# The first map's softmax sum is taken out in the merge's norm; one vector operation combines the two maps

## The chip, the core and the metric

The kernel runs on one core of a Trainium2 chip. The core has a matrix engine (TensorE, PE in the profile), a vector engine (DVE), a scalar engine (ACT), GpSimd (POOL), and a sync engine (SP) whose queue issues every transfer of this kernel. The metric is the device time of one execution in microseconds. Before the change it was 1486.08 us, the median of three runs (1483.74 to 1489.56).

## What is computed

One step of one encoder layer, for a prompt of 1024 frames and for a sample of 32 frames with 512 cached ones. Both go through one input projection, then through two branches, gated linear attention (GLA) and differential attention, and are merged. Differential attention has 8 heads with two maps each; in each map a query of 64 numbers meets keys of 64, and the second map is subtracted with a learned weight `lam`:

```python
def diff_attend(q, k, v, mask, lam):
    s = jnp.einsum('bqhmd,bkhmd->bhmqk', q, k).astype(F32) * (DIFF_HD ** -0.5)
    if mask is not None:
        s = jnp.where(mask, s, -jnp.inf)
    p = jax.nn.softmax(s, axis=-1)
    attn = p[:, :, 0] - lam * p[:, :, 1]
    return jnp.einsum('bhqk,bkhe->bqhe', attn, v.astype(F32))
```

Each head's output then goes through an RMS norm over its 128 channels, and only after that is it multiplied by its gate:

```python
def rmsnorm(x, g):
    xf = x.astype(F32)
    y = xf * lax.rsqrt(jnp.mean(xf * xf, axis=-1, keepdims=True) + EPS) * g.astype(F32)
    return y.astype(x.dtype)
yd = (rmsnorm(o_diff, diff_subln_g) * (1.0 - lambda_init)) * silu(dg)
merged = sigmoid(ma) * (yg @ w_proj_gla) + sigmoid(mb) * (yd @ w_proj_diff)
```

A factor that all channels of one frame of one head share drops out of this norm, except for the small `EPS`.

## The kernel before

Frames and channels are tiled by 128. Every float matmul of a projection is done as three products of rounded parts (high times high, low times high, high times low), so a block of 128 output channels is 3 chunks of 352 frames with 24 matmuls each, 72 in all. The program runs in stages: the norm and the value projections; GLA; differential attention; the merge (projection of the GLA branch, called PG, projection of the attention branch, called PD, and the output projection).

In the two attention stages the blocks of the input projection serve as **fill**: `fill` (L444) hands out six matmuls at a time (L461 to L463) wherever the attention must wait. The order of PE's instructions is made at build time by the class `Order` (L62): each step has a cost, needs with latencies (the table `W`, L52), and PSUM banks; of the threads the first whose step is ready is taken. The latencies are constants, and none is measured while the kernel runs. The instructions of the other engines are put in order by the framework, by priority.

For each head `diff_main` (L896) runs over 8 query tiles i of 128 frames; tile i has w = 128 (i+1) keys. `diff_scores` (L865) makes the scores of both maps (`ps_s`, L879 and L880), their maxima (L883), and the exponentials with their row sums on ACT (L885, sums in the two columns of `sm`). DVE then inverts both sums (L888), multiplies the second map by its inverse and by -lam (L889, over w columns), and multiplies the first map by its inverse and adds the second (L890, over w columns). The result `p` is ready for PE after the latency `soft + W["p"] + w * W["p_w"]` (L894). PE transposes it in groups of up to four 128x128 blocks (`ps_t`, L927; one PSUM bank, freed by the copies L929 and L930), and every second tile multiplies it with the values (`po`, L940 to L942). The row sums before are used up by this; the outputs `osb` and their squares `sqo` are kept.

`diff_fin` (L851) ends a head: the mean square over channels by a matmul (`ps_m`, L855), its store to `msd` (L858), the gate (L861) and the store to `ydd` (L862). The norm itself is applied in the merge: `msd` is loaded as `rs` (L1127), turned into an inverse root by Ln and Exp (L1128, L1129), stored to `rsd` (L1130), loaded as a broadcast `rsb` for two heads at a time (L1136) and multiplied onto the tiles `ydr` (L1137), which are then split into high and low parts `Y` (L1065, L1066) for PD (L439 to L441).

The sample's 32 frames are a thread of their own, `sample_thread` (L950), in four groups of two heads: scores (`ps_ss`, L982), two transposes (`ps_st`, L1002: four blocks, then a remainder of 32 columns), products (`po_s`, L1014), a scaling (`os_`, L1021) and an output transpose (`ps_so`, L1025). The two kinds of transposes share one PSUM bank. The first two blocks of PG are computed together in steps over the tiles `ygr` as they are loaded and split into `y` (`pg_first`, L1081; L1095 to L1097).

Of the kernel before, what the change touches and what calls it, by code (L numbers as in the profile page):

```python
# [11 lines left out]
F32 = mybir.dt.float32  # L12
F32R = mybir.dt.float32r
I32 = mybir.dt.int32
AF = mybir.ActivationFunctionType
ALU = mybir.AluOpType
# [4 lines left out]
P = 128  # L21
NP = 1024
# [6 lines left out]
DH, HD = 8, 64  # L29
NQ = NP // P  # L30
EPS = 1e-6
# [24 lines left out]
    "tr_t": 2.27, "dv": 5.65, "at": 2.45, "pv_o": 1.1, "sdg": 1.84, "sdk": 21.35, "kc": 7.45, "ss_s": 3.69,  # L56
    "sp": 7.1, "st_t": 1.14, "sv": 3.44, "spt": 0.43, "so_o": 3.58, "so": 4.1, "so_t": 0.72, "yg0": 4.48,
    "yg": 1.18, "pg_b": 1.72, "sm": 1.98, "sm_w": 0.00141, "sm_s": 2.25, "p": 2.4, "p_w": 0.00204,
}


# [61 lines left out]
def hybrid_step_kernel(ctx: ExitStack, tc: tile.TileContext, a):  # L123
    nc = tc.nc
    mm = nc.tensor.matmul
    act = nc.scalar.activation
    ve = nc.vector
    dma = nc.sync.dma_start
    st = nc.sync.dma_start
# [4 lines left out]
    dram = ctx.enter_context(tc.tile_pool(name="dram", bufs=1, space=DRAM))  # L134
# [10 lines left out]
    def tbank(name):  # L145
        return pp.tile([P, 512], F32, tag="t", name=name)
# [5 lines left out]
    ident = cst.tile([P, P], F32, name="ident")  # L152
    make_identity(nc, ident)
    eps = cst.tile([P, 1], F32, name="eps")
# [23 lines left out]
    ptd = dram.tile([KT, P, T], F32, name="ptd")  # L178

    msd = dram.tile([DH, NP], F32, name="msd")  # L180
    rsd = dram.tile([DH, NP], F32, name="rsd")


# [146 lines left out]
    with tc.manual_schedule(engines={E.PE, E.Activation, E.DVE, E.Pool}):  # L330
# [25 lines left out]
        ps = bank("ps_v")  # L356
# [400 lines left out]
    dp = pool("dp", reuse_waits="tile")  # L757
# [19 lines left out]
    def sam(n, h):  # L777
        return smp[:, 20 + 4 * n + h % 4, :]

    dqs, dks, dsg = {}, {}, {}  # L780

    def parts(n, cnt):
# [82 lines left out]
    def diff_scores(h, i, out):  # L865
        w = (i + 1) * P
        qsl = slice(i * P, i * P + P)
        qs, (ks, kls) = dqs[h], dks[h]
        sm = dp.tile([P, 2], F32, tag="sm", bufs=2, name="sm")
        pt = []  # L870
        soft = W["sm"] + w * W["sm_w"]
        for m in range(2):
            cost = sum(max(0.11, min(512, w - n0) / 2200) for n0 in range(0, w, 512)) * 2
            yield cost, [(("dk", h), W["dk"]), (("dq", h), W["dq"])], ["s"]
            ps = dbank("ps_s")

            for n0 in range(0, w, 512):
                n = min(512, w - n0)
                mm(ps[:, n0 : n0 + n], qs[m][:, qsl], ks[m][:, n0 : n0 + n], start=True, stop=False)  # L879
                mm(ps[:, n0 : n0 + n], qs[m][:, qsl], kls[m][:, n0 : n0 + n], start=False, stop=True)  # L880
            ve.memset(ps[0:64, w - 64 : w], -1e30)  # L881
            nm = dp.tile([P, 1], F32, tag=f"nm{m}", bufs=2, name="nm")
            ve.tensor_reduce(nm, ps[:, 0:w], axis=AX.X, op=ALU.max, negate=True)  # L883
            p = dp.tile([P, NP], F32, tag=f"p{m}", bufs=2 - m, name="p")
            act(p[:, 0:w], ps[:, 0:w], AF.Exp, bias=nm, accum_out=sm[:, m : m + 1])  # L885
            S.free("s", soft + W["sm_s"])
            pt.append(p)
        ve.reciprocal(sm, sm)  # L888
        ve.tensor_scalar(pt[1][:, 0:w], pt[1][:, 0:w], sm[:, 1:2], neglam, op0=ALU.mult, op1=ALU.mult)  # L889
        ve.scalar_tensor_tensor(pt[0][:, 0:w], pt[0][:, 0:w], sm[:, 0:1], pt[1][:, 0:w], op0=ALU.mult, op1=ALU.add)  # L890
        S.mark(("p", h, i))
        if i == NQ - 1:
            S.mark(("qk", h))
        out[i] = pt[0], soft + W["p"] + w * W["p_w"]  # L894

    def diff_main():  # L896
        fin = None
        for h in range(DH):
            att = {}
            yield 0.0, [(("dq", h), 0.0), (("dk", h), 0.0)], []  # L900
            yield from diff_scores(h, 0, att)
            if fin is not None:
                yield from fin
            vr = tp.tile([P, NQ, P], F32, tag="sg1", name="vr")
            dma(vr, a["newv"][0:NP, h * P : h * P + P].rearrange("(c p) e -> p c e", p=P))
            vh = dp.tile([P, NQ, P], F32R, tag="vh", name="vh")
            vl = dp.tile([P, NQ, P], F32R, tag="vl", name="vl")
            act(vh, vr, AF.Copy)
            nc.gpsimd.tensor_tensor(vl, vr, vh.bitcast(F32), op=ALU.subtract)
            S.mark(("dv", h))  # L910
            osb = tp.tile([P, NP], F32, tag="o", name="osb")
            sqo = rp.tile([P, NP], F32, tag="gst", name="sqo")
            for i in range(NQ):
                g = i // 2
                if i + 1 < NQ:
                    yield from diff_scores(h, i + 1, att)
                p, lat = att.pop(i)
                if i % 2 == 0:
                    ah = dp.tile([P, NQ, 256], F32R, tag="ah", name="ah")
                    al = dp.tile([P, NQ, 256], F32R, tag="al", name="al")  # L920
                dsl = slice((i % 2) * P, (i % 2) * P + P)
                for j0 in range(0, i + 1, 4):
                    nj = min(4, i + 1 - j0)
                    yield 0.11 * nj, [(("p", h, i), lat)], ["t"]
                    ps = tbank("ps_t")
                    for j in range(j0, j0 + nj):
                        nc.tensor.transpose(ps[:, (j - j0) * P : (j - j0 + 1) * P], p[:, j * P : j * P + P], ident)  # L927
                    pv = ps[:, : nj * P].rearrange("p (c s) -> p c s", s=P)
                    act(ah[:, j0 : j0 + nj, dsl], pv, AF.Copy)  # L929
                    ve.tensor_tensor(al[:, j0 : j0 + nj, dsl], pv, ah[:, j0 : j0 + nj, dsl].bitcast(F32),  # L930
                                     op=ALU.subtract)
                    S.free("t", W["tr_t"])
                S.mark(("at", h, i))
                if i % 2 == 0:
                    continue
                yield 0.32 * (i + 0.5), [(("at", h, i), W["at"]), (("dv", h), W["dv"])], ["o"]
                po = obank("po")[:, 0:256]
                for j in range(i + 1):
                    cs = slice(0, 256) if j < i else slice(P, 256)
                    mm(po[:, cs], vh[:, j, :], ah[:, j, cs], start=(j == 0), stop=False)  # L940
                    mm(po[:, cs], vh[:, j, :], al[:, j, cs], start=False, stop=False)  # L941
                    mm(po[:, cs], vl[:, j, :], ah[:, j, cs], start=False, stop=(j == i))  # L942
                act(sqo[:, g * 256 : g * 256 + 256], po, AF.Square)
                act(osb[:, g * 256 : g * 256 + 256], po, AF.Copy)
                S.free("o", W["pv_o"])
                S.mark(("pv", h, g))
            fin = diff_fin(h, osb, sqo)
        yield from fin

    def sample_thread():  # L950
        w = PAST + NS
# [171 lines left out]
    Y = x_pair("Y")  # L1123
    yd = [Y[k // 6][:, k % 6] for k in range(KT)]

    rs = cp.tile([DH, NP], F32, tag="cwh", name="rs")
    dma(rs, msd)  # L1127
    act(rs, rs, AF.Ln, bias=eps[0:DH])  # L1128
    act(rs, rs, AF.Exp, scale=-0.5)  # L1129
    st(rsd, rs)  # L1130
    rsb = {}
# [165 lines left out]
```

## Time and profile before

| | |
|---|---|
| median of three runs | 1486.08 us |
| the profiled execution | 1489.96 us, of it the span 1488.2 us |
| granted PE clock, mean | 0.989 |
| DVE, ACT, POOL busy in the span | 53%, 40%, 20% |
| transfers | 156.58 MB, 32% of the 16 engines' time |
| differential attention on PE | some 605 to 1188 us of the span |
| the merge's first projection (PG) | some 1189 to 1290 us |

The profile is of one execution. Its page has the busy time of each engine, the span in slices, the chain of work that ended last, and the costliest groups of instructions; the trace behind it can be asked for timelines and windows of time. Matmuls overlap: one of 352 columns is listed with some 0.32 us, and the next one starts some 0.16 us after it. An idle time before an instruction is listed with the instruction that ended it.

### The profile page before, as it was taken

How to read it: one execution, taken by the hardware profiler on the slowest of the kernel's cores; microseconds unless marked ns; L12 is line 12 of the kernel's file. 1: busy time of each engine (PE TensorE's matmuls, PEld its weight loads, DVE VectorE, ACT ScalarE, POOL GpSimd, SP SyncE). 2: the span in 40 equal slices, each digit the busy share in tenths (PEclk: the TensorE clock that was granted, in tenths of full speed). 3: DMA queues.
4: the chain of work that ended last, by engine and by line, in shares of the span. 5: the costliest groups of instructions: out<-in, count | busy, mean ns of one | idle time of the engine just before them, and what ended most of it. 6: DMA issues, size and time to landing. Idle time of an engine off the chain costs nothing.

```text
span 1488.2 us, 22365 instructions
## 1 busy us (share of the span) xinstructions
PE 1427.6 (96%) x8848; PEld 1330.4 (89%) x8848; DVE 790.4 (53%) x1464; ACT 600.5 (40%) x1262; POOL 298.4 (20%) x186
## 2 busy tenths in 40 slices
PE   8999999998989999899999999999899899999997
PEld 6787778988989899899989998999799789999997
DVE  5612004565565443576767676768665536455415
ACT  4522114445444233355555555555454432221311
POOL 1200002132312133222222322222221111121001
PEclk9999999999999999999999999999999999999999
DMA  8621111122222134313141323233322278643205
GB/s 295 215 99 38 44 43 45 52 74 70 75 89 66 66 101 124 102 47 119 52 115 62 108 74 105 64 100 85 97 62 86 91 264 311 215 135 127 100 1 191
DMA packets 66742, 156.58 MB, mean 105 GB/s; under 512 B 10008, under 2 KB 28568, under 8 KB 65600
## 3 DMA queue, kind: packets, MB, share of 16 engines
q1 hardware_dynamic: 66624, 155.01, 32.2%
q8 instruction: 74, 1.21, 0.3%
q14 instruction: 44, 0.36, 0.1%
HBM read 104.39 MB, written 40.04 MB: 97 GB/s over the span
## 4 chain that ended last, share of the span: by engine, by line
PE 51%; DVE 5%; DMA 4%; ACT 2%; issue 1%; POOL 1%; SPq 0%; DVEq 0%; POOLq 0%; ACTq 0%
PE ps_w L461 9%; PE ps_w L462 9%; PE ps_w L463 9%; PE ps_w L440 2%; PE ps_w L439 2%; PE ps_w L441 2%; PE ps_c L1189 2%; PE ps_c L1191 2%; PE ps_c L1190 2%; PE ps_s L880 2%; PE ps_t L927 2%; PE ps_s L879 2%; DMA ydr<-ydd 1%; PE po L941 1%; PE po L942 1%
## 5 line engine op out<-in xcount | busy, mean ns | idle before, releaser
L461 PE MATMUL ps_w<-X,wh 128*128 128x352 f32 x1344 | 451.8, 336 | 8.4 <-ACT k L492 3.2
L462 PE MATMUL ps_w<-X,wl 128*128 128x352 f32 x1344 | 437.4, 325 | 0.0
L463 PE MATMUL ps_w<-X,wh 128*128 128x352 f32 x1344 | 435.5, 324 | 0.0
L431 POOL TENSOR_TENSOR wl<-wr,wh 128x1024 fp32r<-128x1024 f32 x72 | 178.5, 2479 | 659.6 <-ACT wh L429 535.9
L461 PEld LDWEIGHTS ps_w<-X,wh 128*128 128x128 f32 x1344 | 255.3, 190 | 13.5 <-issue 4.8
L462 PEld LDWEIGHTS ps_w<-X,wl 128*128 128x128 f32 x1344 | 255.3, 190 | 1.2 <-issue 1.2
L463 PEld LDWEIGHTS ps_w<-X,wh 128*128 128x128 f32 x1344 | 256.0, 190 | 0.0
L885 ACT ACTIVATE p<-ps_s,nm 128x256 f32<-128x256 f32 (+7 forms) x128 | 94.6, 741 | 58.7 <-DVE ps_s L881 31.0
L286 PE MATMUL ps_v<-wh,X 128*128 128x512 f32 x248 | 98.1, 396 | 1.9 <-DVE X L225 1.9
L285 PE MATMUL ps_v<-wh,X 128*128 128x512 f32 x248 | 99.5, 401 | 0.0
L287 PE MATMUL ps_v<-wl,X 128*128 128x512 f32 x248 | 98.9, 399 | 0.0
L429 ACT ACTIVATE wh<-wr 128x1024 fp32r<-128x1024 f32 x72 | 75.8, 1053 | 55.1 <-PE ps_w L463 30.4
L883 DVE TENSOR_REDUCE nm<-ps_s 128x1 f32<-128x256 f32 (+7 forms) x128 | 94.7, 746 | 2.7
L272 DVE TENSOR_TENSOR vo<-ps_v,vo 32x512 f32<-32x512 f32 x4 | 2.7, 678 | 141.7 <-ACT vo L271 141.7
L881 DVE MEMSET ps_s<- 64x64 f32 x128 | 14.3, 112 | 114.7 <-PE ps_s L880 113.1
L646 POOL TENSOR_TENSOR vl<-vr,vh 128x512 fp32r<-128x512 f32 (+1 forms) x20 | 24.8, 1238 | 223.9 <-ACT vh L645 223.9
L879 PE MATMUL ps_s<-k,q 128*128 128x512 f32 (+2 forms) x192 | 68.0, 362 | 1.2 <-DMA k<-k 1.2
L880 PE MATMUL ps_s<-kl,q 128*128 128x512 f32 (+2 forms) x192 | 63.9, 348 | 3.7 <-DMA kl<-kl 3.2
L268 ACT ACTIVATE vo<-ps_v 128x512 f32<-128x512 f32 x32 | 19.1, 596 | 116.5 <-PE ps_v L287 115.6
L929 ACT ACTIVATE ah<-ps_t 128x512 fp32r<-128x512 f32 (+2 forms) x96 | 46.9, 488 | 43.8 <-PE ps_t L927 43.1
L930 DVE TENSOR_TENSOR al<-ps_t,ah 128x512 fp32r<-128x512 f32 (+2 forms) x96 | 53.1, 553 | 18.7 <-ACT ah L929 17.4
L440 PE MATMUL ps_w<-Y,wl 128*128 128x352 f32 x192 | 62.3, 324 | 0.0
(319 smaller groups left out, 2971.0 us busy)
## 6 DMA issues: line engine op xcount, KB each, us to landing
wr<-w SPq DMA_DIRECT2D x72, 512.0 KB
thd<-gate SPq DMA_DIRECT2D x16, 528.0 KB
xn<-xn SPq DMA_DIRECT2D x16, 512.0 KB
wr<-wv SPq DMA_DIRECT2D x16, 512.0 KB
newk<-rr SPq DMA_DIRECT2D x8, 528.0 KB
ygr<-ygd SPq DMA_DIRECT2D x8, 528.0 KB
tha<-thd SPq DMA_DIRECT2D x8, 528.0 KB
ydr<-ydd SPq DMA_DIRECT2D x8, 528.0 KB
```

The source lines that it names most:

```text
L285: mm(ps, xk[:, 0, t0 : t0 + P], wh[:, k, :], start=(k == 0), stop=False)
L286: mm(ps, xk[:, 1, t0 : t0 + P], wh[:, k, :], start=False, stop=False)
L287: mm(ps, xk[:, 0, t0 : t0 + P], wl[:, k, :], start=False, stop=(k == KT - 1))
L431: nc.gpsimd.tensor_tensor(wl, wr, wh.bitcast(F32), op=ALU.subtract)
L440: mm(ps[:, :n], wl[:, k, :], src[k][:, 0, t0 : t0 + n], start=False, stop=False)
L461: mm(ps[:, :n], wh[:, k, :], src[k][:, 0, t0 : t0 + n], start=(k == 0), stop=False)
L462: mm(ps[:, :n], wl[:, k, :], src[k][:, 0, t0 : t0 + n], start=False, stop=False)
L463: mm(ps[:, :n], wh[:, k, :], src[k][:, 1, t0 : t0 + n], start=False, stop=(k == KT - 1))
L879: mm(ps[:, n0 : n0 + n], qs[m][:, qsl], ks[m][:, n0 : n0 + n], start=True, stop=False)
L880: mm(ps[:, n0 : n0 + n], qs[m][:, qsl], kls[m][:, n0 : n0 + n], start=False, stop=True)
L883: ve.tensor_reduce(nm, ps[:, 0:w], axis=AX.X, op=ALU.max, negate=True)
L885: act(p[:, 0:w], ps[:, 0:w], AF.Exp, bias=nm, accum_out=sm[:, m : m + 1])
```

## The change

The exponentials of the first map are no longer divided by their sum. The second map is scaled by -lam times the first map's sum over its own, a number for each frame, and one operation multiplies and adds. What goes to the values is therefore the old map times the first map's sum s0, and so is the head's output. The sums s0 of all heads and tiles are gathered in the 64 columns of one tile `s0a`, transposed at the end of the attention, and stored. In the merge the mean square (s0 squared times the old one) gets EPS times s0 squared in place of EPS, which makes the norm's result the old one. The sample is computed as before. Two numbers of the planner's table change: the latency from the exponentials to the transposes.

```diff
-    ... "p": 2.4, "p_w": 0.00204,
+    ... "p": 2.2, "p_w": 0.00145,
...
+    s0d = dram.tile([DH, NP], F32, name="s0d")
...
+    s0a = tp.tile([P, DH * NQ], F32, name="s0a")
+    s0t = tp.tile([DH * NQ, P], F32, name="s0t")
...
-        sm = dp.tile([P, 2], F32, tag="sm", bufs=2, name="sm")
+        sm = dp.tile([P, 1], F32, tag="sm", bufs=2, name="sm")
+        s0 = s0a[:, h * NQ + i : h * NQ + i + 1]
...
-            act(p[:, 0:w], ps[:, 0:w], AF.Exp, bias=nm, accum_out=sm[:, m : m + 1])
+            act(p[:, 0:w], ps[:, 0:w], AF.Exp, bias=nm, accum_out=sm if m else s0)
...
         ve.reciprocal(sm, sm)
-        ve.tensor_scalar(pt[1][:, 0:w], pt[1][:, 0:w], sm[:, 1:2], neglam, op0=ALU.mult, op1=ALU.mult)
-        ve.scalar_tensor_tensor(pt[0][:, 0:w], pt[0][:, 0:w], sm[:, 0:1], pt[1][:, 0:w], op0=ALU.mult, op1=ALU.add)
+        ve.scalar_tensor_tensor(sm, sm, neglam, s0, op0=ALU.mult, op1=ALU.mult)
+        ve.scalar_tensor_tensor(pt[0][:, 0:w], pt[1][:, 0:w], sm, pt[0][:, 0:w], op0=ALU.mult, op1=ALU.add)
...
         yield from fin
+        yield 0.11, [], ["t"]
+        ps = tbank("ps_s0")
+        nc.tensor.transpose(ps[0 : DH * NQ, 0:P], s0a, ident)
+        act(s0t, ps[0 : DH * NQ, 0:P], AF.Copy)
+        S.free("t", W["tr_t"])
+        st(s0d.rearrange("h (i q) -> (h i) q", q=P), s0t)
...
-    rs = cp.tile([DH, NP], F32, tag="cwh", name="rs")
+    rs2 = cp.tile([DH, 2, NP], F32, tag="cwh", name="rs")
+    rs, s0 = rs2[:, 0], rs2[:, 1]
     dma(rs, msd)
-    act(rs, rs, AF.Ln, bias=eps[0:DH])
+    dma(s0, s0d)
+    ve.scalar_tensor_tensor(s0, s0, EPS, s0, op0=ALU.mult, op1=ALU.mult)
+    ve.tensor_tensor(rs, rs, s0, op=ALU.add)
+    act(rs, rs, AF.Ln)
     act(rs, rs, AF.Exp, scale=-0.5)
```

With the two numbers of the table the order of PE's instructions changes. Three places follow. Line numbers of the changed kernel are higher: L462 to L464 are the fill (before L461 to L463), L1013 the sample's transposes (before L1002).

The first is on PE, at the end of the sixth head and the start of the seventh, for the third group of the sample. Before, its two transposes (`ps_st`) stood there with six fill matmuls and a mean-square matmul between them:

```order
L879 MATMUL ps_s<-k_11286,q_10924 128x128
L880 MATMUL ps_s<-kl_11288,q_10924 128x128
L1002 MATMUL ps_st<-ident,p 128x128 x4
L461 MATMUL ps_w<-X_89,wh 128x352
L462 MATMUL ps_w<-X_89,wl 128x352
L463 MATMUL ps_w<-X_89,wh 128x352
L461 MATMUL ps_w<-X_89,wh 128x352
L462 MATMUL ps_w<-X_89,wl 128x352
L463 MATMUL ps_w<-X_89,wh 128x352
L855 MATMUL ps_m<-sqo,one_h 128x512
L1002 MATMUL ps_st<-ident,p 32x128
```

Now, for the same group, the second transpose stands behind the last product of the seventh head and the next head's first scores:

```order
L947 MATMUL po<-ah,vl 128x256
L945 MATMUL po<-ah,vh 128x128
L946 MATMUL po<-al,vh 128x128
L947 MATMUL po<-ah,vl 128x128
L883 MATMUL ps_s<-k_12105,q_11699 128x128
L884 MATMUL ps_s<-kl_12107,q_11699 128x128
L883 MATMUL ps_s<-k_12106,q_11700 128x128
L884 MATMUL ps_s<-kl_12108,q_11700 128x128
L1013 MATMUL ps_st<-ident,p 32x128
L462 MATMUL ps_w<-X_89,wh 128x352
```

The first transpose of that group (four blocks) now stands 79 rows ahead of this one, before the last tile's transposes of the seventh head.

The second place is on PE too, at the end of the last head. Before, the transposes of its last tile (`ps_t`, eight blocks) stood between the products of the sample, and the head's last product (`po`) followed at once, without fill:

```order
L463 MATMUL ps_w<-X_89,wh 128x352
L1002 MATMUL ps_st<-ident,p 32x128
L1014 MATMUL po_s<-vcs,smp 32x128 x4
L1015 MATMUL po_s<-smp 32x128
L927 MATMUL ps_t<-ident,p 128x128 x8
L1014 MATMUL po_s<-vcs,smp 32x128 x4
L1015 MATMUL po_s<-smp 32x128
L940 MATMUL po<-ah,vh 128x256
```

Now fill steps stand between those transposes (18 matmuls behind each four blocks), and behind the last product (L945 to L947) there is fill as well, with the sample's last transposes:

```order
L945 MATMUL po<-ah,vh 128x128
L946 MATMUL po<-al,vh 128x128
L947 MATMUL po<-ah,vl 128x128
L1013 MATMUL ps_st<-ident,p 128x128 x4
L462 MATMUL ps_w<-X_89,wh 128x352
L463 MATMUL ps_w<-X_89,wl 128x352
L858 MATMUL ps_m<-sqo,one_h 128x512
L464 MATMUL ps_w<-X_89,wh 128x352
```

The last group's products and output now stand among the first matmuls of the merge.

The third place is the queue of SP in the merge. The norms' way (`rs`, `rsd`, `rsb`) stands among weight loads (`wr`), stores of finished PG blocks (`ptd`) and loads of gates (`tha`). Before:

```order
L1127 DMA rs<-msd 8x1024
L1062 DMA ydr<-ydd 128x1056 x2
L1102 DMA ptd<-tha 128x1056
L427 DMA wr<-w 128x1024
L1130 DMA rsd<-rs 8x1024
L1102 DMA ptd<-tha 128x1056
L1074 DMA tha<-thd 128x1056
L427 DMA wr<-w 128x1024
L1074 DMA tha<-thd 128x1056
L1136 DMA rsb<-rsd 128x2048
```

Now, with the weight load of PG's fourth block already issued ahead of these rows:

```order
L1139 DMA rs<-msd 8x1024
L1085 DMA tha<-thd 128x1056
L1113 DMA ptd<-tha 128x1056
L428 DMA wr<-w 128x1024
L1140 DMA rs<-s0d 8x1024
L1085 DMA tha<-thd 128x1056
L1073 DMA ydr<-ydd 128x1056 x2
L1122 DMA ptd<-tha 128x1056
L1085 DMA tha<-thd 128x1056
L428 DMA wr<-w 128x1024
L1145 DMA rsd<-rs 8x1024
L1151 DMA rsb<-rsd 128x2048
```

The first broadcast stands behind the store of PG's third block and the weight load of the sixth block; before it stood behind the store of the second and the weight load of the fifth.

More of the change, by code (lines that the diff above doesn't have):

```diff
@@ L57 @@
     "sp": 7.1, "st_t": 1.14, "sv": 3.44, "spt": 0.43, "so_o": 3.58, "so": 4.1, "so_t": 0.72, "yg0": 4.48,
-    "yg": 1.18, "pg_b": 1.72, "sm": 1.98, "sm_w": 0.00141, "sm_s": 2.25, "p": 2.4, "p_w": 0.00204,
+    "yg": 1.18, "pg_b": 1.72, "sm": 1.98, "sm_w": 0.00141, "sm_s": 2.25, "p": 2.2, "p_w": 0.00145,
 }
```

## The prediction, made before the changed kernel ran

> **What bounds the kernel now.** The page's first part comes first: the busy time of each engine and its share of the span.
>
> ```profile
> PE 1427.6 (96%) x8848; PEld 1330.4 (89%) x8848; DVE 790.4 (53%) x1464; ACT 600.5 (40%) x1262; POOL 298.4 (20%) x186
> ```
>
> TensorE (PE) is busy 96% of a span of 1488.2 us, so a faster vector engine (DVE) can only shorten the times in which PE stands still for it. The second view is the table of windows, over the three stages that the change reaches: the differential attention of the prompt, the change-over to the merge, and the first projection of the merge. Columns: window, length, then busy time and instructions of PE, weight loads, DVE, ACT, POOL, then the granted clock, the DMA share and GB/s.
>
> ```profile
> 610.00:1180.00 570.00, 558.51 (x3583) 528.95 (x3584) 392.20 (x775) 298.05 (x687) 135.76 (x63) 1.00 0.27 80
> 1180.00:1215.00 35.00, 28.18 (x169) 24.97 (x170) 14.79 (x18) 13.51 (x20) 3.08 (x3) 1.00 0.75 258
> 1215.00:1300.00 85.00, 84.24 (x519) 82.94 (x518) 43.05 (x47) 23.77 (x25) 19.08 (x8) 1.00 0.73 266
> ```
>
> PE stands still for 570 - 558.51 = 11.5 us in the attention, 35 - 28.18 = 6.8 us in the change-over and 0.8 us in the projection, with the clock at 1.00. DVE is busy only 392 of 570 us. About 19 us is all that this change can win; its arithmetic on PE stays as it is. The timeline of PE then says where these 19 us lie (start, duration, instruction; in brackets the idle time before it and what ended it).
>
> ```profile
> 754.67 0.28 PE L1002 MATMUL ps_st<-ident,p 128*32 128x128 f32 x1 [1.27 <-DVE smp L1005]
> 792.16 0.33 PE L927 MATMUL ps_t<-ident,p 128*128 128x128 f32 x1 [1.33 <-DVE al L930]
> 1034.99 0.66 PE L927 MATMUL ps_t<-ident,p 128*128 128x128 f32 x4 [1.32 <-DVE al L930]
> 1046.41 0.27 PE L1002 MATMUL ps_st<-ident,p 128*32 128x128 f32 x1 [2.33 <-DVE smp L1005]
> 1073.90 0.63 PE L927 MATMUL ps_t<-ident,p 128*128 128x128 f32 x4 [1.68 <-DVE smp L1028]
> 1181.95 0.66 PE L927 MATMUL ps_t<-ident,p 128*128 128x128 f32 x4 [1.41 <-DVE al L930]
> 1184.29 0.39 PE L940 MATMUL po<-ah,vh 128*128 128x256 f32 x1 [0.36 <-ACT os__13006 L1016]
> 1189.06 0.43 PE L1095 MATMUL ps_w<-y,wh 128*128 128x352 f32 x1 [1.52 <-ACT y L1065]
> 1190.58 0.43 PE L1097 MATMUL ps_w<-y,wh 128*128 128x352 f32 x1 [0.93 <-DVE y L1066]
> 1195.57 0.43 PE L1095 MATMUL ps_w<-y,wh 128*128 128x352 f32 x1 [1.29 <-ACT y L1065]
> 1196.86 0.43 PE L1097 MATMUL ps_w<-y,wh 128*128 128x352 f32 x1 [0.70 <-DVE y L1066]
> ```
>
> None of these rows waits for the two operations that the change edits (L889, L890). The long ones wait for a one-bank transpose buffer that a late DVE operation holds, mostly around the sample's steps (L1002, L1005, L1028), and at the change-over for the loads of the merge.
>
> **The edit on DVE.** The groups by line (count, busy us, mean ns) and three rows of the DVE timeline give its price.
>
> ```profile
> L890 DVE SCALAR_TENSOR_TENSOR p<-p,sm 128x128 f32<-128x128 f32 (+3 forms) x64 | 56.5, 883 | 1.8
> L889 DVE TENSOR_SCALAR p<-p,sm,neglam 128x128 f32<-128x128 f32 (+3 forms) x64 | 43.0, 672 | 1.8
> L888 DVE RECIPROCAL sm<-sm 128x2 f32<-128x2 f32 x64 | 10.4, 163 | 18.1 <-ACT p L885 17.2
> L995 DVE TENSOR_TENSOR r<-r,coef 128x1 f32<-128x1 f32 x4 | 0.9, 233 | 0.1
> ...
> 1046.19 0.33 DVE L889 TENSOR_SCALAR p<-p,sm,neglam 128x128 f32<-128x128 f32 x1
> 1046.55 0.35 DVE L890 SCALAR_TENSOR_TENSOR p<-p,sm 128x128 f32<-128x128 f32 x1
> 1091.64 0.75 DVE L889 TENSOR_SCALAR p<-p,sm,neglam 128x896 f32<-128x896 f32 x1
> ```
>
> Removed: 64 tensor_scalar, 43.0 us. Added: 64 scalar_tensor_tensor on one column, which the trace does not show. Bounds: the reciprocal of two columns, 163 ns, and the 128-column form of the same operation, 0.35 us. I take 233 ns, the one-column tensor_tensor, the nearest in shape and operands: 64 x 0.233 = 14.9 us. DVE is relieved by 43.0 - 14.9 = 28.1 us (20.6 to 32.6). The wide operation that stays keeps its 56.5 us, and the reciprocal its price. The probabilities of a tile are ready earlier by 0.33 - 0.23 = 0.1 us at 128 columns and 0.5 us at 896. Of the 28 us almost nothing lies on the path, since PE has fill matmuls to run meanwhile.
>
> Whether the freed operation ever held DVE up longer shows beside POOL:
>
> ```profile
> 1060.68 2.47 POOL L796 TENSOR_TENSOR sw<-sw,stb 128x1056 f32<-128x1056 f32 x1
> 1060.74 2.50 DVE L1021 TENSOR_SCALAR os__11629<-os__11629,ss 64x128 f32<-64x128 f32 x1 [0.66 <-POOL ss L162]
> 1185.51 0.28 DVE L1021 TENSOR_SCALAR os__13006<-os__13006,ss 64x128 f32<-64x128 f32 x1 [0.66 <-POOL ss L162]
> ```
>
> The same small operation takes 2.50 us beside a POOL operation and 0.28 us alone. [...]
>
> **The order on PE.** The two planner numbers for the latency of the probabilities fall by 0.28 us at 128 columns and 0.80 us at 1024. In each head one fill step of six matmuls leaves the inside of the head, eight in all, to be used later; the sample's steps move too. What that does, term by term:
>
> - The sample's two transposes no longer stand close to each other in the first three groups: many matmuls come between. The waits of 1.27 and 2.33 us go: -3.6 us.
> - At the end of the last head, fill steps now stand between the transposes and behind the last product. The 1.41 us, and 0.36 us for the sample's output, go: -1.7 us.
> - The 1.32 us at 1034.99 comes from a DVE queue that also carries the splits of k. The sample's scores no longer stand there; I count half: -0.7 us.
> - The backlogs around the sample's outputs (1.33, 1.68 us and smaller ones; what remains of the 11.5 us apart from the terms above is 6.6 us) recur in three heads after the change as before. The last such head has no rotation left for POOL and DVE. A shorter queue takes somewhat over a quarter: -1.8 us (0 to -6.6).
> - At the change-over the waits of 1.52, 0.93, 1.29 and 0.70 us remain: the same loads, conversions and splits precede the first product of the merge. The fill moved there covers about 2 us, but the store of the last gate and a weight conversion now stand ahead of the merge's second and third tiles on the sync engine's queue and on ACT. I count 0 (-4.4 to +2).
> - New waits: transposes now come one fill step earlier behind their scores. The narrowest tile of those shows what is left:
>
> ```profile
> 855.47 0.89 DVE L890 SCALAR_TENSOR_TENSOR p<-p,sm 128x640 f32<-128x640 f32 x1
> 858.45 0.60 PE L927 MATMUL ps_t<-ident,p 128*128 128x128 f32 x4
> ```
>
>  The slack is 858.45 - 856.36 = 2.1 us. One fill step is six matmuls; by the two rows under "rivals" one matmul costs 0.16 us, so the transposes come 0.97 us earlier, and 1.1 us stays even without the edit. In two heads the sample's transposes now stand just ahead of the last tile's and hold the one bank. I count +2.0 us for all new waits (0 to +4).
> - The transpose of the sums, one matmul with its bank: +0.3 us. Its copy on ACT and its store have no one waiting nearby.
>
> The sum is -3.6 - 1.7 - 0.7 - 1.8 + 0 + 2.0 + 0.3 = **-5.5 us**.
>
> **The norm in the merge.** Two more loads and vector operations stand ahead of the broadcast of the norms, and the sync engine now issues it behind the weights of a block that is one later. The rows of before:
>
> ```profile
> 1207.49 0.32 SPq L1127 DMA_DIRECT2D rs<-msd  x1
> 1216.05 1.15 ACT L1128 ACTIVATE rs<-rs,eps 8x1024 f32<-8x1024 f32 x1
> 1218.51 1.06 ACT L1129 ACTIVATE rs<-rs 8x1024 f32<-8x1024 f32 x1
> 1225.32 0.38 SPq L1136 DMA_DIRECT2D rsb<-rsd  x1
> 1273.01 1.25 DVE L1066 TENSOR_TENSOR Y<-ydr,Y 128x1056 fp32r<-128x1056 f32 x1
> 1289.93 0.32 PE L439 MATMUL ps_w<-Y,wh 128*128 128x352 f32 x1
> ```
>
> The last tile is split at 1274.3 and used at 1289.9: a cover of 15.6 us. A block is 72 matmuls, 11.6 us. The two added operations are bounded by nothing and by 1.25 us each (the split of 1056 columns). The last tile is then ready at 1285.9 to 1288.4, still 1.5 to 4 us early. Price: nothing, with little cover left.
>
> **Rivals.** (1) The waits only change their place. The planner's numbers fall by some 0.2 us more than the edit saves, and each new order meets POOL's 2.4 us operations at other points. For it: the waits above come from chance meetings; against it: the two longest go by the order alone. It gives -1 us, 1485. (2) The relief of DVE clears nearly all waits for it: -3.6 - 1.7 - 1.3 - 6.6 = -13 us, 1473. Against it: L1021 and the conversions of the merge do not change. (3) Slower: the norm comes a second block late. If the first broadcast misses one more weight load on the sync engine's queue, the last tile is ready at 1297.5 to 1300, PE waits 7.6 to 10 us ahead of the second projection, and the time is 1486.1 - 5.5 + 10 = 1490.6, or 1495 if the waits above remain. It decides from a delay of 15.6 us; I count 11.6 to 14.1. (4) The change doesn't do what it says: all sums lie in one tile, and if each exponential had to wait for the last use of that tile on DVE, 64 tiles would each lose up to 0.5 us, 1486.1 - 5.5 + 32 = 1513. Against it: in the built program the first map's exponential waits for DVE at the same counts as before. (5) PE is not the bound at all:
>
> ```profile
> 1025.88 0.32 PE L463 MATMUL ps_w<-X,wh 128*128 128x352 f32 x1
> 1029.72 0.32 PE L463 MATMUL ps_w<-X,wh 128*128 128x352 f32 x1
> ```
>
> If PE had hidden room as large as the idle time of the weight loads in the attention (570 - 528.95 = 41 us), all of DVE's 28.1 us could come out: 1458. Between these two rows lie 24 starts in 3.84 us, 0.16 us each, at half the duration of a matmul: the stream is dense. [...]
>
> **How the numbers follow.** The profiled execution took 1489.96 us (its span and 1.8 us around it), 3.9 us over the median of 1486.08. The terms are differences made in that execution: 1484.5 for it, and 1486.1 - 5.5 = 1480.6, so 1481, on the median. Chances: forecast (1477.5 to 1483) 0.42, rival 1 0.24, rival 2 0.18, rival 3 0.11, rival 4 0.03, rival 5 0.02. The range 1471 to 1492 takes in rivals 1 and 2 and most of 3 and leaves out the rest. A measurement of this kernel tells about 0.5%, 7.4 us, from no change: faster than 1478.7 are rivals 2 and 5 and a quarter of the forecast, 0.31; slower than 1493.5 are half of rival 3 and rival 4, 0.09; between them 0.60.
>
> **What would show it.** In the changed kernel's timeline of PE the sample's second transposes should have no wait in front, the last head's transposes no wait over 0.5 us, and the first four waits of the merge should still sum to 3 to 5 us. DVE's busy time should fall by 20 to 33 us, the one-column operation take 0.16 to 0.35 us. The window 610 to 1180 should show some 5 us of idle PE less. A wait of PE for Y ahead of the second projection would be rival 3. The forecast is wrong if new waits over 1 us stand in the heads around the sample's outputs, or if the merge's first tiles come later than counted.

## The result and the profile after

The changed kernel takes **1502.43 us** (median of 4 runs, 1501.49 to 1504.63); the kernel before took 1486.00 us beside it. The ratio is 1.0103, its 95% interval 1.0078 to 1.0128: slower by 1%. The forecast was 1481, its range 1471 to 1492.

The first part of the page of the changed kernel, with its span, to be held against that of before:

```profile
span 1501.1 us, 22384 instructions
PE 1434.7 (96%) x8849; PEld 1337.4 (89%) x8849; DVE 761.6 (51%) x1466; ACT 599.1 (40%) x1263; POOL 296.8 (20%) x186
```

DVE has 28.8 us less to do, as the change promises. PE has one instruction more and yet is busy 7.1 us longer, and the span is 12.9 us longer. So PE stood still longer (5.8 us of the span), and something made its instructions slower. The windows of the attention and of the change-over show both (columns as before: PE, weight loads, DVE, ACT, POOL, then the granted clock):

```profile
610.00:1190.00 580.00, 560.13 (x3549) 531.39 (x3549) 365.47 (x774) 295.36 (x681) 133.95 (x63) 0.98 0.27 78
1190.00:1225.00 35.00, 31.92 (x185) 27.53 (x184) 14.66 (x16) 13.35 (x23) 3.04 (x2) 0.95 0.66 220
```

In the attention PE now stands still for 19.9 us, where it was 11.5, and the granted clock is 0.98 in place of 1.00. The timeline of PE says where (the idle time ahead of an instruction and its releaser in brackets):

```profile
782.04 0.34 PE L1036 MATMUL ps_so<-ident,os__8566 64*128 64x64 f32 x1 [3.80 <-DVE os__8566 L1032]
857.16 0.63 PE L932 MATMUL ps_t<-ident,p 128*128 128x128 f32 x4 [1.15 <-DVE ps_s L885]
927.90 0.63 PE L932 MATMUL ps_t<-ident,p 128*128 128x128 f32 x4 [1.15 <-DVE ps_s L885]
961.71 1.08 PE L932 MATMUL ps_t<-ident,p 128*128 128x128 f32 x4 [5.05 <-DVE smp L1016]
1044.35 0.30 PE L883 MATMUL ps_s<-k,q 128*128 128x128 f32 x1 [1.56 <-ACT osb L949]
1046.78 0.30 PE L884 MATMUL ps_s<-kl,q 128*128 128x128 f32 x1 [2.12 <-DMA kl<-kl]
1122.94 0.47 PE L884 MATMUL ps_s<-kl,q 128*128 128x128 f32 x1 [2.16 <-DMA kl<-kl]
1200.12 0.43 PE L1106 MATMUL ps_w<-y,wh 128*128 128x352 f32 x1 [1.41 <-ACT y L1076]
```

None of the waits of before that the prediction quoted from 750 to 1182 us is there; in their place stand seven new ones of 17.0 us in all (the first seven rows). The two longest wait for the sample's operations on DVE, two for the remainders of K (`kl`, its low parts) at the start of a head. What the longest wait leaves behind it shows in windows of 2 us; the last three numbers are the clock, the DMA share and GB/s:

```profile
778.00:780.00 2.00, 0.24 (x3) 0.10 (x1) 1.94 (x3) 0.94 (x3) 1.57 (x1) 1.00 0.66 270
780.00:782.00 2.00, 0.00 (x0) 0.00 (x0) 1.90 (x2) 0.00 (x0) 1.02 (x1) 0.78 0.00 0
782.00:784.00 2.00, 1.96 (x7) 1.87 (x8) 0.41 (x2) 0.00 (x0) 0.00 (x0) 0.50 0.84 253
784.00:786.00 2.00, 2.00 (x8) 1.71 (x7) 0.17 (x2) 0.00 (x0) 0.00 (x0) 0.50 0.13 26
786.00:788.00 2.00, 2.00 (x10) 1.90 (x9) 1.79 (x3) 0.12 (x1) 0.00 (x0) 0.51 0.00 0
788.00:790.00 2.00, 2.00 (x14) 2.00 (x13) 0.87 (x2) 2.00 (x4) 0.00 (x0) 1.00 0.00 0
```

PE resumes at 782.0 with the clock at 0.50 and starts 7 to 10 instructions in 2 us where it starts 14 at full clock. Summed as (1 - clock) x 2 us over these rows, 3.4 us are lost, all but 0.4 of them on top of the wait. Such a stretch is called a **fall** below, and what it loses its loss.

Why the 5.05 us? ACT's row for the sample's transposes, and DVE's timeline behind it:

```profile
954.76 0.39 ACT L1015 ACTIVATE smp<-ps_st 128x256 f32<-128x256 f32 x1 [2.80 <-PE ps_st L1013]
```

```profile
953.02 2.76 DVE L801 TENSOR_TENSOR rr<-rr,ct 128x352 f32<-128x352 f32 x3
...
956.67 0.95 DVE L803 TENSOR_TENSOR rr<-rr,sw 128x352 f32<-128x352 f32 x2
957.54 0.41 DVE L834 TENSOR_TENSOR kl<-rr,k 64x256 fp32r<-64x256 f32 x1
...
960.68 0.42 DVE L835 TENSOR_TENSOR kl<-rr,k 64x256 fp32r<-64x256 f32 x1
961.14 0.42 DVE L1016 TENSOR_TENSOR smp<-ps_st,smp 128x256 f32<-128x256 f32 x1
```

The sample's first transposes (954.12 on PE) now come 8 us after the end of the K projection of the next head, just when the rotation of that K reaches DVE. ACT has copied its half by 955.15, but DVE's add (L1016) is queued behind the whole rotation (L801 to L803) and split (L834, L835) of that K, and the bank that it holds is the only one for transposes. The 3.80 us have the same form: the sample's scaling L1032, ready after 773.7, stands behind the next tile's steps, among them four splits of q and one combination of probabilities that takes 2.85 us beside a POOL operation (0.89 us for the same form at 707.74, with none beside it; DVE's timeline, then POOL's):

```profile
778.86 2.85 DVE L895 SCALAR_TENSOR_TENSOR p<-p,sm 128x640 f32<-128x640 f32 x1
781.63 0.27 DVE L1032 TENSOR_SCALAR os__8566<-os__8566,ss 64x128 f32<-64x128 f32 x1
```

```profile
778.43 2.59 POOL L432 TENSOR_TENSOR wl<-wr,wh 128x1024 fp32r<-128x1024 f32 x1 [4.70 <-ACT wh L430]
```

### The profile page after: what moved, and what is told of

The parts are those of the page before. It is cut to its first block, busy times and chain, and to the rows that moved or that the text cites. A ratio compares the mean times of both kernels' runs of the same rounds, so it can differ in the third digit from the quotient of the medians.

```text
span 1501.1 us, 22384 instructions
## 1 busy us (share of the span) xinstructions
PE 1434.7 (96%) x8849; PEld 1337.4 (89%) x8849; DVE 761.6 (51%) x1466; ACT 599.1 (40%) x1263; POOL 296.8 (20%) x186
## 3 DMA queue, kind: packets, MB, share of 16 engines
q8 instruction: 74, 1.21, 0.3%
## 4 chain that ended last, share of the span: by engine, by line
PE 53%; DVE 6%; DMA 4%; ACT 2%; issue 1%; POOL 1%; SPq 0%; DVEq 0%; POOLq 0%; ACTq 0%
PE ps_w L462 9%; PE ps_w L463 9%; PE ps_w L464 9%; PE ps_s L884 2%; PE ps_s L883 2%; PE ps_w L441 2%; PE ps_w L440 2%; PE ps_w L442 2%; PE ps_t L932 2%; PE ps_c L1206 2%; PE ps_c L1204 2%; PE ps_c L1205 2%; DMA kl<-kl 1%; PE po L946 1%; PE ps_m L858 1%; PE po L947 1%
## 5 line engine op out<-in xcount | busy, mean ns | idle before, releaser
L462 PE MATMUL ps_w<-X,wh 128*128 128x352 f32 x1344 | 454.2, 338 | 8.5 <-ACT k L493 3.2
L463 PE MATMUL ps_w<-X,wl 128*128 128x352 f32 x1344 | 438.0, 326 | 0.0
L464 PE MATMUL ps_w<-X,wh 128*128 128x352 f32 x1344 | 436.9, 325 | 0.0
L432 POOL TENSOR_TENSOR wl<-wr,wh 128x1024 fp32r<-128x1024 f32 x72 | 175.2, 2433 | 621.2 <-ACT wh L430 557.3
L462 PEld LDWEIGHTS ps_w<-X,wh 128*128 128x128 f32 x1344 | 256.5, 191 | 14.4 <-issue 5.7
L463 PEld LDWEIGHTS ps_w<-X,wl 128*128 128x128 f32 x1344 | 256.5, 191 | 1.8 <-issue 1.7
L464 PEld LDWEIGHTS ps_w<-X,wh 128*128 128x128 f32 x1344 | 256.7, 191 | 0.2 <-issue 0.2
L440 PE MATMUL ps_w<-Y,wh 128*128 128x352 f32 x192 | 61.7, 321 | 0.0
```

The lines of the kernel that those rows point to most:

```text
L432: nc.gpsimd.tensor_tensor(wl, wr, wh.bitcast(F32), op=ALU.subtract)
L462: mm(ps[:, :n], wh[:, k, :], src[k][:, 0, t0 : t0 + n], start=(k == 0), stop=False)
L463: mm(ps[:, :n], wl[:, k, :], src[k][:, 0, t0 : t0 + n], start=False, stop=False)
L464: mm(ps[:, :n], wh[:, k, :], src[k][:, 1, t0 : t0 + n], start=False, stop=(k == KT - 1))
```

## Experiments

Three theories are told apart. A: the new order of PE, made by the two planner numbers, costs the time, by new waits. B: the new arithmetic costs it. C, beside either: each long wait of PE is followed by a fall of the clock, so that it costs more than it lasts.

**Order or arithmetic.** The first two kernels take the change apart: e1 is the kernel before with the two planner numbers, e2 the changed kernel without them.

```diff
 e1, in the kernel before:
-"p": 2.4, "p_w": 0.00204,
+"p": 2.2, "p_w": 0.00145,
 e2, in the changed kernel: the same lines the other way round
```

> The kernel before with the two planner numbers alone (p 2.2, p_w 0.00145); both maps are still scaled as before. Its TensorE order is that of the changed kernel row for row, save the transpose of the sums. Theory A (the order costs the time): the waits of 3.8 us (sample's output transpose) and 5.05 us (last tile's transposes behind the sample's add) and those for the K remainders stand here too, each followed by a stretch at half clock: 1498 to 1510 us. Theory B (the new arithmetic costs it): 1483 to 1489 us, as before. If 1490 to 1497, each has a part of it.

> The changed kernel with the old planner numbers (p 2.4, p_w 0.00204); the arithmetic, the transpose of the sums and the norm's three added steps in the merge are in. Its TensorE order is that of before row for row, with one transpose more. Theory A: no wait over 3 us between 610 and 1190 us, VectorE busy near 762 us, 1478 to 1488 us. Theory B: 1498 to 1505 us, with the waits of the changed kernel.

Measured: e1 1512.28 us, ratio 1.0176 (1.0160 to 1.0191); e2 1485.83 us, ratio 1.0006 (0.9992 to 1.0019). The mechanism of theory A holds in both, though e1 lies 2 us above its range: the order alone costs 26 us, and the arithmetic is worth nothing in the old order. In the new order it is worth 10 us (1512.3 to 1502.4): the waits of e1 are the same ones, longer (4.92 us in place of 3.80, 2.36 and 2.38 in place of 1.15), apart from that of 5.05 us, which stands there unchanged, and one of 1.56 us at 961 us more. A shorter DVE queue helped only where PE waited for that queue.

**The two long waits.** e3 takes the sample's add and its scaling away from DVE's queue, in the changed kernel:

```diff
-ve.tensor_tensor(pT[0:kw, c0 : c0 + n], pv[:, :, :, 1, :], pT[0:kw, c0 : c0 + n], op=ALU.add)
+p2 = p[0:kw, 0 : n * 64].rearrange("p (c h t) -> p c h t", h=2, t=NS)
+act(p2, pv[:, :, :, 1, :], AF.Copy)
+ve.tensor_tensor(pT[0:kw, c0 : c0 + n], p2, pT[0:kw, c0 : c0 + n], op=ALU.add)
...
-ve.tensor_scalar(os_, os_, ss, None, op0=ALU.mult)
+act(os_, os_, AF.Copy, scale=ss)
```

> The changed kernel and its numbers, with two operations of the sample's thread taken off VectorE's queue: its second map is copied out of the transposes' bank by ScalarE, so that the bank is free before VectorE adds, and its output is scaled by ScalarE. Theory A with its price (wait and the half clock behind it): the waits of 3.80 and 5.05 us go, and with them two stretches of 6.8 us at half clock (3.4 us each): 1502.4 - 8.9 - 6.8 = 1486.7, range 1484 to 1492. Rival (the half clock has nothing to do with the waits): 1502.4 - 8.9 = 1493.5, range 1492 to 1496. Rival (the waits only change place): 1498 to 1504 us.

Measured: 1491.77 us, ratio 1.0029 (1.0012 to 1.0046). Both waits are gone, and with them both falls. Of the 10.7 us won only 8.9 could be the waits themselves. By its time alone e3 (1484.67 to 1497.85) doesn't tell theory A from the first rival, whose range begins at 1492; the trace does, in which the losses behind 610 us are 6.8 us less. It stays 5 us short of the forecast. Some 3 us of that are new waits, of which two of 1.30 and 1.15 us at 780 and 965 us are the first: PE's idle time is 5.7 us less, not 8.9. The rest is not explained. The waits for K are left.

**K earlier.** e6 and e8 are e3 with a larger constant for the time from a K projection to its use:

```diff
-"dk": 14.32,
+"dk": 20,        (e6)     "dk": 16.5,      (e8)
```

> The run with two waits off (new arithmetic, new numbers p and p_w), with the planner's time from the end of a K projection to its use raised from 14.32 to 20 (traced: 19.6 us from the end of the projection to the landing of the K remainders at 1046.8 in the changed kernel). Theory A: the heads no longer wait for the K remainders (2.12 and 2.17 us at 1036 and 1112, with 1.7 and 3.4 us of half clock), nor 1.58 us for the output's gate ahead of one of them: 1491.8 - 5.9 - 5.1 = 1481, range 1478 to 1487. Rival (the whole order moves again, new waits elsewhere): 1488 to 1500 us.

> As the run with the new order and the early K, but with 16.5 in place of 20 for the planner's time from the K projection to its use. With 20 the fill steps ran out ahead of the merge, which then waited 7.84 us for its first Y tile with 5.1 us of half clock, and the run still took 1481.0 us; with 16.5 the last head keeps two fill steps for that place. Theory A: the wait for Y is 1.4 us again and the heads' waits for K stay under 1 us: 1481 - 6.4 - 3.4 = 1471, range 1470 to 1480. Rival (with 16.5 K comes late again in some heads): 1482 to 1492 us.

Measured: e6 1480.99 us, ratio 0.9975 (0.9962 to 0.9988); e8 1480.34 us, ratio 0.9971 (0.9952 to 0.9990). From the changed kernel to e8 22.1 us are won, and e8 is 1.1 us from the same arithmetic and edit in the old order (e5, below): with the two operations and the constant for K the whole price of the new order is gone. The constant moves the steps of the order once more, so how much of it is the waits for K alone is not isolated. In e6 all waits for K went, as forecast, but that its time came out is partly luck: the waits of 1.23 and 2.21 us ahead of the first head went too, with 3.4 us of losses, and the wait of 7.83 us at the merge came, with losses of 5.1 us, and neither had been counted. The forecast for e8 did not come out: in place of e6's one wait of 7.83 us at the merge e8 has two of 2.36 and 1.99 us, and others of 1.1 to 1.9 us in the heads; PE's idle time is only 1.9 us less. The rows of PE in e6 (first) and e8:

```profile
1177.16 0.66 PE L1108 MATMUL ps_w<-y,wh 128*128 128x352 f32 x1 [7.83 <-ACT y L1078]
```

```profile
1176.06 0.43 PE L1108 MATMUL ps_w<-y,wh 128*128 128x352 f32 x1 [2.36 <-ACT y L1078]
1178.64 0.66 PE L1110 MATMUL ps_w<-y,wh 128*128 128x352 f32 x1 [1.99 <-DVE y L1079]
```

**The old order with the two operations off.** e5 is e2 with e3's edit, e10 the kernel before with it, e7 is e5 with "dk" 20.

> The new arithmetic with the old planner numbers, and the sample's two operations taken off VectorE's queue as in the run with two waits off. In the run of the arithmetic alone the sample's second transposes waited 1.27 and 2.33 us for VectorE's add, with 1.7 us of half clock behind the second. Theory A: these go, 1485.8 - 3.6 - 1.7 = 1480.5 us, range 1478 to 1484. Rival (they change place): 1484.5 to 1489 us.

> The kernel before, its arithmetic and its order, with the sample's two operations taken off VectorE's queue. It tells whether the new arithmetic is worth anything once those waits are gone (the run of the old order with two off: 1479.2 us). Theory (VectorE's saved 28 us lie beside TensorE): 1478 to 1481 us, the same as that run. Rival (the saved vector time shows as soon as the sample's waits don't hide it): 1482 to 1486 us.

> The kernel with the new arithmetic, the old numbers p and p_w and the two operations off VectorE's queue, and the planner's time for K raised from 14.32 to 20 as well. Its order differs from that of before only in where the sample's groups stand. Theory A: as the run before it in this list without the larger time, 1478 to 1484 us, since the old order has no wait for K behind the first head. Rival: over 1487 us.

Measured: e5 1479.22 us, ratio 0.9964 (0.9948 to 0.9980), the lowest median of all; e10 1480.79 us, 0.9969 (0.9952 to 0.9986), both as forecast. The small edit to the sample beats both kernels, and the new arithmetic adds nothing to it that these runs can tell: DVE's 28 us lie beside PE. e7 came out as its rival has it: 1497.41 us, ratio 1.0075 (1.0056 to 1.0094). Its profiled execution took 1504.64 us, 7.2 us over the median. In its last head the sample's transposes and products stand next to each other, with no fill step between. The window there, with PE at 13.75 of 20 us and the clock at 0.66:

```profile
1180.00:1200.00 20.00, 13.75 (x63) 10.01 (x61) 5.50 (x10) 7.07 (x18) 2.89 (x2) 0.66 0.28 107
```

**Is it enough to tell the planner?** e11 leaves the changed kernel's operations alone and sets three constants to the traced times.

```diff
-"dk": 14.32, "st_t": 1.14, "so": 4.1,
+"dk": 19.6,  "st_t": 6.8,  "so": 13.7,
```

> The changed kernel with three of the planner's constants set to what its trace shows and nothing else edited: the sample's transposes hold their bank for 6.8 us (954.7 to 961.6; the table has 1.14), the sample's output is scaled 13.7 us after its products (768.2 to 781.9; the table has 4.1), K is ready 19.6 us after its projection (1027.2 to 1046.8; the table has 14.32). Theory A (the new order hurts because steps stand as close as constants allow that are too short): the waits of 3.80, 5.05, 2.12 and 2.16 us go with their half clock, 1478 to 1487 us. Rival (longer constants only move the waits, since they also use the fill steps up sooner): 1490 to 1505 us.

Measured: 1503.44 us, ratio 1.0118 (1.0096 to 1.0140). The rival holds: the four named waits are gone, but three of 3.90 us behind the sample's output (L1039) and two of 2.31 us for L1016 have come. A delay that depends on what DVE happens to have in its queue was not met by these constants; taking the operation out of that queue did meet it.

**The price of a wait.** e4 and e9 put seven waits of rising length into the dense second projection of the merge of the changed kernel; e9 also holds PE's order there as it is written.

```diff
+lens = [0, 1, 3, 5, 8, 11, 15, 20]
...
+pg = tbank("ps_g")
+nc.tensor.transpose(pg[:, 0:P], gpost[:, 0:P], ident)
+for g in range(lens[j]):
+    act(d, pg[:, 0:P] if g == 0 else d, AF.Copy)
+pg = tbank("ps_g")
+nc.tensor.transpose(pg[:, 0:P], d, ident)
```

> The changed kernel with seven waits made on purpose in the merge's second projection, where TensorE otherwise runs without a gap: ahead of each of the blocks 1 to 7 TensorE transposes a tile that ScalarE has first copied 1, 3, 5, 8, 11, 15 and 20 times in turn, about 1 to 7 us of idle TensorE. The copies change nothing that is read later. Theory C (the half clock is what a wait leaves behind it): behind waits up to about 1.5 us the granted clock stays 1.00; behind those of 2 to 3.4 us it falls to 0.50 in some places, for 3.4 us (1.7 us lost); behind those over 3.4 us always, for 3.4 or 6.8 us (1.7 or 3.4 us lost). Rival (the clock falls for another reason, such as power, DMA or the time since the last fall): no connection with the seven places. The time would be 1502.4 + the seven waits (about 25 us) + 7 to 17 us of half clock under C, and 1502.4 + the waits alone under the rival.

> The seven waits made on purpose once more; in the run before, the order of TensorE was free in that stage, the transposes were moved to where they had nothing to wait for, and only one wait of 0.94 us stood. Now the order is held as written, so that each wait stands at its block. Theory C: behind waits up to about 1.5 us the granted clock stays 1.00; behind 2 to 3.4 us it falls to 0.50 in some places, for 3.4 us; behind over 3.4 us always, for 3.4 or 6.8 us. Rival: no connection with the seven places. The waits should be 1.5 to 7.5 us.

e4 failed as an experiment: the framework moved the transposes, only waits of 0.94, 0.69 and 0.45 us were left, and it took 1504.36 us (two runs), ratio 1.0124 (1.0093 to 1.0156). e9 took 1536.69 us (two runs), ratio 1.0335 (1.0294 to 1.0376). PE's timeline shows five of its waits, from the third to the last, and windows behind three of them the clock:

```profile
1342.65 0.33 PE L1165 MATMUL ps_g<-ident,gap 128*128 128x128 f32 x1 [2.17 <-ACT gap L1163]
1358.56 0.33 PE L1165 MATMUL ps_g<-ident,gap 128*128 128x128 f32 x1 [3.19 <-ACT gap L1163]
1377.02 0.48 PE L1165 MATMUL ps_g<-ident,gap 128*128 128x128 f32 x1 [4.21 <-ACT gap L1163]
1397.95 0.47 PE L1165 MATMUL ps_g<-ident,gap 128*128 128x128 f32 x1 [5.57 <-ACT gap L1163]
1419.52 0.48 PE L1165 MATMUL ps_g<-ident,gap 128*128 128x128 f32 x1 [6.45 <-ACT gap L1163]
```

```profile
1341.00:1347.00 6.00, 4.35 (x27) 4.35 (x28) 2.36 (x2) 1.50 (x5) 2.50 (x2) 1.00 0.69 229
1357.00:1363.00 6.00, 4.44 (x18) 4.45 (x19) 1.52 (x1) 1.38 (x5) 1.38 (x2) 0.72 0.69 253
1375.00:1383.00 8.00, 5.98 (x21) 5.98 (x22) 0.97 (x1) 1.81 (x6) 0.82 (x2) 0.57 0.48 170
```

Behind 1.46, 1.48 and 2.17 us the clock stays at 1.00. Behind 3.19 us 1.7 us are lost ((1 - 0.72) x 6), behind 4.21, 5.57 and 6.45 us 3.4 us each. The seven waits are 24.5 us and these losses 11.9: 1502.4 + 24.5 + 11.9 = 1538.8 us, against 1526.9 for the waits alone, and 1536.69 was measured. Theory C holds.

With this the times of the runs without made waits can be put together: the span of each profiled execution, PE's idle time between its instructions, and the losses of all falls but the one in the last microseconds, each summed over 1 us windows.

| kernel | span | idle PE | losses | the rest |
|---|---|---|---|---|
| before | 1488.2 | 51.8 | 13.6 | 1422.8 |
| changed | 1501.1 | 57.4 | 23.9 | 1419.8 |
| e1 numbers alone | 1511.2 | 64.9 | 23.9 | 1422.4 |
| e2 arithmetic alone | 1483.9 | 48.9 | 12.0 | 1423.0 |
| e3 two waits off | 1491.3 | 51.7 | 18.8 | 1420.8 |
| e5 old order, two off | 1476.3 | 48.1 | 6.8 | 1421.4 |
| e6 new order, K earliest | 1482.6 | 48.5 | 15.4 | 1418.7 |
| e7 old order, K earliest | 1502.9 | 60.2 | 18.8 | 1423.9 |
| e8 new order, K earlier | 1477.8 | 46.7 | 6.8 | 1424.3 |
| e10 before, two off | 1478.0 | 44.4 | 12.0 | 1421.6 |
| e11 planner told | 1503.3 | 56.0 | 27.3 | 1420.0 |

The rest is the same within 5.6 us in kernels that differ by 35 us. The time of this kernel is its matmuls, the waits of PE, and what the clock loses behind them. From before to the change the waits grow by 5.6 us and the losses by 10.3; some 3 us of the losses lie inside waits and are counted twice, so 12.9 are seen. The 10.3 understate the change. Up to 643 us PE's order is the same row for row in both kernels, and the losses before 610 us, 13.6 and 10.2 us, can't differ by the change. Behind 610 us there are none before the change and 13.7 us after it. So the profiled execution of before lies 3.9 us over its median, and that of the change 0.5 us over its own: the spans differ by 12.9 us, the medians by 16.4.

## Why the prediction was wrong

- **The bound** was read rightly: PE is the bound, and DVE's relief is worth 28.8 us of DVE and nothing in time in the old order (e2).
- **The price of the edit** was off in its parts. The one-column operation cost 372 ns in the mean, not 233, above both bounds:

```profile
L895 DVE SCALAR_TENSOR_TENSOR p<-p,sm 128x128 f32<-128x128 f32 (+3 forms) x64 | 58.6, 916 | 2.0
L894 DVE SCALAR_TENSOR_TENSOR sm<-sm,neglam,s0a 128x1 f32<-128x1 f32 x64 | 23.8, 372 | 2.0
```

  Its median is 220 ns; eight of the 64 took 0.56 to 2.53 us, each beside a POOL operation, in the longest case for the whole of it:

```profile
625.30 2.53 DVE L894 SCALAR_TENSOR_TENSOR sm<-sm,neglam,s0a 128x1 f32<-128x1 f32 x1
```

```profile
625.35 2.47 POOL L799 TENSOR_TENSOR sw<-sw,stb 128x1056 f32<-128x1056 f32 x1 [1.28 <-DVE sm L892]
```

  So the removed line less the added one gave 43.0 - 23.8 = 19.2 us, below the bounds too. That the total of 28.8 lies within the forecast 20 to 33 is luck: other lines met POOL less often. The sample's scaling fell from 7.7 to 1.1 us: before, three of its four took 2.47 to 2.50 us beside a POOL operation, after the change all four took 0.27 to 0.28 with none. The scaling in the merge fell from 15.9 to 10.8: before, four of its eight took 2.66 to 3.00 us beside one, after it one, 2.42 us; the others took 1.21 to 1.23.
- **The terms that go** went: the sample's second transposes (-3.6), the last head's end (-1.7) and the 1.32 us (-0.7, counted by half) have no wait any more. But the 1.27 and 2.33 us had waited for the sample's add, and so do the new 5.05 us: it is the next user of the same bank that now waits. At the change-over 1.41, 0.70, 0.27 and 0.71 us are left, 3.1 us, within the 3 to 5 that were named.
- **The backlogs around the sample's outputs** (-1.8) were not shortened by a shorter queue. In e2, with the old order, they stand much as before: 1.46 and 1.50 us where there were 1.33 and 1.32, and 1.27 and 2.33 us unchanged; only the 1.68 us fell, to 1.38. In the new order the sample's output has the 3.80 us instead.

```profile
747.50 0.28 PE L1013 MATMUL ps_st<-ident,p 128*32 128x128 f32 x1 [1.27 <-DVE smp L1016]
784.44 0.33 PE L932 MATMUL ps_t<-ident,p 128*128 128x128 f32 x1 [1.46 <-DVE al L935]
1026.22 0.66 PE L932 MATMUL ps_t<-ident,p 128*128 128x128 f32 x4 [1.50 <-DVE al L935]
1037.61 0.37 PE L1013 MATMUL ps_st<-ident,p 128*32 128x128 f32 x1 [2.33 <-DVE sm L894]
```

- **New waits, "+2.0 us for all new waits (0 to +4)"**, is the step that failed. The prediction named the place ("just ahead of the last tile's and hold the one bank") and priced it by the slack of the narrowest tile, 2.1 us. It did not ask what DVE has ahead of the sample's add there, a whole rotation of K, nor did it follow the K projection, which the order also moved. The waits are 17.0 us; e3 and, with what was said of it, e6 show that they carry the loss. The sign of being wrong that the prediction gave, new waits over 1 us around the sample's outputs, is there (3.80 us). For the wait of 2.12 us: before, the rotation of that K began 29 us ahead of the head's first scores (1012.2 to 1041.2), now 17 us (to 1044.35); the rows of SP's queue in the changed kernel:

```profile
1027.44 0.64 SPq L797 DMA_DIRECT2D sw<-rr  x1
...
1042.55 1.39 SPq L838 DMA_DIRECT2D kl<-kl  x2
```

- **The clock was left out of the sum**, a second miss of nearly the same size: 13.7 us of losses in the stages that the change reaches, where there were none. The profile of before had shown the effect outside the windows that the prediction chose: they begin at 610 us, and rounding to 1.00 over 570 us hid the rest. A window of the kernel before, behind its waits of 1.22 and 2.21 us, which end at 606.5 and 609.0 us:

```profile
608.00:616.00 8.00, 6.56 (x23) 6.43 (x24) 1.68 (x7) 0.92 (x4) 0.00 (x0) 0.57 0.33 91
```

- **The rivals.** Rival 1 (waits only change place) had the mechanism and not the size. Rival 3 did not come: the norm chain is late as counted and still in time, 2.85 us ahead of its use (forecast 1.5 to 4):

```profile
1298.63 1.25 DVE L1077 TENSOR_TENSOR Y<-ydr,Y 128x1056 fp32r<-128x1056 f32 x1
...
1302.73 0.32 PE L440 MATMUL ps_w<-Y,wh 128*128 128x352 f32 x1
```

  Against rivals 2 and 5 (the relief shows) stands e2, which is not faster. Rival 4 did not come either: the exponentials wait for the maxima, and ACT is idle less ahead of them than before (58.7 us there):

```profile
L889 ACT ACTIVATE p<-ps_s,nm 128x256 f32<-128x256 f32 (+7 forms) x128 | 94.3, 740 | 23.7 <-DVE nm L887 17.4
```

What stays open: why the orders of e7, e8 and e11 make just those new waits was read from their traces, not tried.

## What to carry to other kernels

Where one engine is the bound and others run beside it, a change of a static order is priced by the queues that the moved steps land behind, on every engine that holds a buffer for the bound one; a saving on a covered engine is priced at nothing until a wait names that engine's queue (e2: DVE busy 369.70 of 570 us in the attention, where it was 392.20, at a ratio of 1.0006). A short dependent operation that releases the only buffer of its kind was better given to another engine than to a later due time here: that edit won 5.5 us (e10) and 6.6 us (e5) in the old order, and truer due times alone won nothing (e11). Waits of the matrix engine of over some 2 us could cost more than their length here (e9: 1.7 us lost behind 3.19, 3.4 behind 4.21, nothing behind 2.17; over twelve profiles a fall behind 9 of 17 waits of 2.0 to 2.6), so one long wait was worth more effort than several short ones of the same sum.

## What the hardware showed that was not expected

In the twelve profiles of before, of the change and of e1 to e10 every fall of the clock after the first 100 us, that of the end apart, follows a wait of PE. Its loss is 1.7 us or a multiple (3.4, once 5.1 and once 6.8). Counted over waits of 0.7 us or more with no other such wait within 3.4 us: 0 of 92 below 1.2 us have a fall behind them, 2 of 60 from 1.2 to 1.7, 6 of 21 from 1.7 to 2.0, 9 of 17 from 2.0 to 2.6, 16 of 21 from 2.6 to 3.3, and 11 of 11 above. One and the same wait of 3.16 to 3.19 us, near 240 us in all twelve, lost nothing three times, 1.7 us five times and 3.4 us four times. So part of what differs between executions of one kernel, and between kernels with equal waits, is chance.

The chance has a form, which the clock's record in the traces shows. In each of the thirteen profiles of this case all falls behind the first 100 us begin on a grid of steps of 3.413 us, all but the last also end on it, and where the grid lies differs from profile to profile. In the changed kernel falls begin at 781.13, 958.62, 1047.37 and 1122.46 us, 52, 26 and 22 steps apart. Counted over the steps at full clock, by PE's idle time within one step: behind less than 1.4 us the next step was never at half clock (0 of 5013), behind 1.4 to 1.7 us in 4 of 37, behind 1.7 to 2.0 in 21 of 28, and above that always (53 of 53). So in these profiles a fall comes when PE was idle for more than about half of one step (1.7 of 3.413 us), and whether a wait of 2 to 3 us does that depends on where the grid cuts it. The wait near 240 us shows it: of its 3.17 us in the changed kernel 1.59 lie in one step and 1.57 in the next, and no fall follows; of its 3.18 us before, 1.93 lie in one step, and 3.4 us are lost.
